# Moving the last four conv-branch tiles of a hybrid trunk layer from the scan's stretch to the Strassen stage ahead of it

## The chip, the cores and the metric

One core of a Trainium2 chip runs the whole program. The metric is the device time of one execution in microseconds (us). TensorE (PE in the rows, its weight loads PEld) multiplies matrices into PSUM; VectorE (DVE), ScalarE (ACT) and GpSimd (POOL) work on tiles of 128 partitions; SyncE (SP) issues most of the loads from memory. Each engine takes its instructions in the order of its own queue.

## The reference, cut to what matters

One layer for 1024 time steps and a model width of 1024, all in float32:

```python
u = rms_norm(x, ln1) * (1 + scale1) + shift1
gl, cb, cc, cx, z, xbc, dt = split(u @ w_in)
y_conv = cb * causal_depthwise_conv(cc * cx, conv_w)       # width 3
p_conv = y_conv @ w_conv_out
xbc = silu(causal_depthwise_conv(xbc, ssm_conv_w) + ssm_conv_b)
xs, bs, cs = split(xbc)                                    # 8 groups
y = ssd_scan(xs * dt, dt * a, bs, cs) + d_skip * xs
y = group_rms_norm(y * silu(z)) * ssm_norm_w
merged = sigmoid(gl_conv) * p_conv + sigmoid(gl_ssm) * (y @ w_ssm_out)
x = x + gate1 * (merged @ w_o)
...
x = x + gate2 * (square(relu(u2 @ w_up)) @ w_down)
```

The conv branch is y_conv: three projections of u (cb, cc, cx, each 1024 channels wide), one product, three taps, one product. In tiles of 128 channels these are eight conv tiles with three projection tiles each.

## The kernel before, in words

Everything lies transposed, channels on partitions and the 1024 time steps along the tile, in two halves of 512. A float32 product is made of three matmuls: each operand is split into a rounded high part (a cast on ScalarE) and the remainder (a subtraction on VectorE), and high x high, high x low and low x high are summed in PSUM. The weights' split is load_w (lines 88 to 95), the three matmuls mm3 (107 to 112), and proj (114 to 121) makes a projection tile of 128 channels from eight blocks of u, 8 x 2 x 3 = 48 matmuls of 512 columns. It takes two of the four PSUM buffers of pool mm.

strassen_pair (134 to 181) makes two projection tiles at once by a Strassen scheme of seven products instead of eight. Each product is 4 blocks x 3 matmuls, so a pair is 84 matmuls where two proj calls are 96. It needs sums of the weights (s12, s34) and of u (the tiles t in X, made once), and hands four quarters of the result, (i, h) for tile i and half h, to a function evac. Their order is (1,1) after four products, (0,0) after five, (0,1) after six and (1,0) after seven.

In order of the program:

1. Norm statistics, modulation, u, and the first six gate tiles (lines 252 to 359).
2. The Strassen stage (425 to 481): ten gate tiles in five pairs, sixteen z tiles in eight pairs, then conv tiles 0 to NYE - 1 = 3. The conv loop at line 456 takes two conv tiles in a round of three pairs: one pair makes cx and cc of the first tile and its product v, one the same for the second, and one makes cb of both. The taps (450 to 454) are one ScalarE and two VectorE instructions. The result lies in two buffers of pool glp (name glt) and is stored to yc_d on ScalarE's queue (481). The tile v has one buffer (name wv), which POOL's memset of two columns opens.
3. The cumulated decays (487 to 506).
4. The scan's stretch (667 to 676). proj_group(g) makes the four projection tiles xs0, xs1, bf and cf of group g through xbc_tile (520 to 532): proj, then raw and cacc with two buffers each, three taps of 1024 columns on VectorE, tanh, one product. ssd_group (546 to 619) runs the scan over eight chunks of 128 steps with small matmuls into A (553 to 556), B (576, 581) and C (598). After the scans of groups 1 to 4, conv_tile (644 to 658) makes conv tiles 4 to 7 with three proj calls each, on tiles ccs and vv of pool pcf, two buffers each, and stores to yc_d.
5. The eight yc_d tiles are reloaded into ccs (683) and split into ys (685), which take the space of u's tiles uh and ul, and so wait for the last projection of group 7. The output projection of the conv branch (693 to 700) runs beside the last scan, then the ssm output projection, w_o, and the MLP.

The engines' orders are not written by hand: a scheduler goes through the program with modelled times and lets an instruction that is ready pass ahead of earlier ones that are not, on each engine. So the projections of group g+1 run on TensorE beside the scan of group g, and the conv tile after them; the scan of group g+1 stands behind both in the program.

Of the kernel before, what the change touches and what calls it, by code (L numbers as in the profile page):

```python
# [5 lines left out]
F32 = mybir.dt.float32  # L6
# [3 lines left out]
ALU = mybir.AluOpType  # L10
# [3 lines left out]
P = 128  # L14
T = 1024
H = 512
# [4 lines left out]
EPS = 1e-6  # L21
RSQRT_SEED = 0x5F3759DF
WARM = 3
NYE = 4
PARTS = ((0, 512, (1, 4, 6)), (512, 256, (1, 3, 4, 6)), (768, 256, (2, 5)))

LN1, LN2, FNORM = 0, 8, 16
# [9 lines left out]
def hybrid_trunk(tc, xT, par, hrows, crow, wada1, wada2, win, wdt, wco, wso, wo, wup, wdn, out):  # L37
    nc = tc.nc
    pe, act, dve, pool, sp = nc.tensor, nc.scalar, nc.vector, nc.gpsimd, nc.sync

    def tt(o, a, b, op, eng=dve):
        return eng.tensor_tensor(out=o, in0=a, in1=b, op=op)  # L42

    def stt(o, a, s, b, op0, op1):
        return dve.scalar_tensor_tensor(out=o, in0=a, scalar=s, in1=b, op0=op0, op1=op1)  # L45
# [4 lines left out]
    hs = [slice(0, H), slice(H, T)]  # L50
# [30 lines left out]
    yc_d = dp.tile([8, P, T], F32, name="yc_d")  # L81

    def load_raw(src):
        raw = wp.tile([P, T], F32, name="wraw", bufs=3)
        sp.dma_start(raw, src)
        return raw

    def load_w(src, raw=None, eng=dve):
        if raw is None:
            raw = load_raw(src)  # L90
        hi = wp.tile([P, T], F32R, name="whi")
        act.copy(hi, raw)  # L92
        lo = wp.tile([P, T], F32R, name="wlo")
        tt(lo, raw, hi.bitcast(F32), ALU.subtract, eng=eng)
        return hi, lo

    def split(hi, lo, src):
        act.copy(hi, src)
        tt(lo, src, hi.bitcast(F32), ALU.subtract)
# [7 lines left out]
    def mm3(outs, wh, wl, xh, xl, start, stop):  # L107
        for o, h_, l_ in zip(outs, xh, xl):
            pe.matmul(o, lhsT=wh, rhs=h_, start=start, stop=False)  # L109
            pe.matmul(o, lhsT=wh, rhs=l_, start=False, stop=False)  # L110
        for o, h_ in zip(outs, xh):
            last_mm[0] = pe.matmul(o, lhsT=wl, rhs=h_, start=False, stop=stop)  # L112

    def proj(w, xh, xl, nk=KT, base=0, halves=(0, 1), width=H):
        wh, wl = w
        ps = [mm.tile([P, H], F32, name="mm")[:, :width] for _ in halves]
        for k in range(nk):
            c0 = base + k * P
            mm3(ps, wh[:, c0:c0 + P], wl[:, c0:c0 + P], [xh[k][h] for h in halves], [xl[k][h] for h in halves],
                k == 0, k == nk - 1)  # L120
        return ps
# [121 lines left out]
    uh = [[up.tile([P, H], F32R, name=f"uh{k}{h}") for h in (0, 1)] for k in range(KT)]  # L243
    ul = [[up.tile([P, H], F32R, name=f"ul{k}{h}") for h in (0, 1)] for k in range(KT)]
# [140 lines left out]
    def sm(name):  # L385
        return p0d.tile([P, C2], F32, name=name)
# [4 lines left out]
    v = sm("v")  # L391
# [58 lines left out]
    def taps(o, v, f):  # L450
        w0 = CONVW + 3 * f
        act.mul(o, v[:, 2:2 + T], prm[:, w0 + 2:w0 + 3])
        for j in (1, 0):
            stt(o, v[:, j:j + T], prm[:, w0 + j:w0 + j + 1], o, ALU.mult, ALU.add)

    for f0 in range(0, NYE, 2):
        ys_ = []
        for f in (f0, f0 + 1):
            y = glp.tile([P, T], F32, name="glt")
            v = pe1.tile([P, T + 32], F32, name="wv", bufs=1)  # L460
            pool.memset(v[:, 0:2], 0.0)
            keep = {}

            def v_ev(i, h, src):
                if (i, h) == (1, 1):
                    keep[0] = src
                elif (i, h) == (0, 0):
                    act.copy(y[:, hs[0]], src)
                else:
                    tt(v[:, 2 + H * h:2 + H * h + H], src, keep[0] if h else y[:, hs[0]], ALU.mult)  # L470

            strassen_pair(pe1, win[17 + 3 * f], win[16 + 3 * f], X, v_ev)
            taps(y, v, f)
            ys_.append(y)

        def y_ev(i, h, src):
            tt(ys_[i][:, hs[h]], src, ys_[i][:, hs[h]], ALU.mult)

        strassen_pair(pe1, win[18 + 3 * f0], win[21 + 3 * f0], X, y_ev)
        for i in (0, 1):  # L480
            act.dma_start(yc_d[f0 + i], ys_[i])
# [5 lines left out]
    with tc.issue_after(last_mm[0].ins):  # L487
# [8 lines left out]
        v = p0e.tile([P, C2], F32, name="v")  # L496
# [18 lines left out]
    pcf = tc.alloc_tile_pool(name="pcf", bufs=2, reuse_waits="tile")  # L515
# [18 lines left out]
    def proj_group(g):  # L534
        pg = p2g[g % 2]
        xs = pg.tile([P, 2, T], F32, name="xs")
        bf = pg.tile([P, T], F32, name="bf")
        cf = pg.tile([P, T], F32, name="cf")
        b = gtile(g)
        xbc_tile(b + 0, 2 * g, xs[:, 0, :])  # L540
        xbc_tile(b + 1, 2 * g + 1, xs[:, 1, :])
        xbc_tile(b + 2, 16 + g, bf)
        xbc_tile(b + 3, 24 + g, cf)
        return xs, bf, cf
# [96 lines left out]
        tsc(r, r, 0.5, None, ALU.mult, ALU.bypass)  # L641
        act.dma_start(rst_d[4 * i:4 * i + 4].rearrange("g (c t) -> (g c) t", t=P), r)

    def conv_tile(f):
        ccs = pcf.tile([P, T], F32, name="ccs")
        v = pcf.tile([P, T + 2], F32, name="vv")
        pool.memset(v[:, 0:2], 0.0)
        cps = proj(load_w(win[16 + 3 * f]), uh, ul)
        for h in (0, 1):
            act.copy(ccs[:, hs[h]], cps[h])  # L650
        xps = proj(load_w(win[17 + 3 * f]), uh, ul)
        for h in (0, 1):
            tt(v[:, 2 + H * h:2 + H * h + H], xps[h], ccs[:, hs[h]], ALU.mult)
        taps(ccs, v, f)
        bps = proj(load_w(win[18 + 3 * f]), uh, ul)
        for h in (0, 1):
            tt(ccs[:, hs[h]], bps[h], ccs[:, hs[h]], ALU.mult)
        act.dma_start(yc_d[f], ccs)

    def drive(gen):  # L660
        try:
            next(gen)
            return None
        except StopIteration as e:
            return e.value
# [3 lines left out]
    for g in range(NG - 1):  # L669
        gen = ssd_group(g, *cur, prev)  # L670
        prev = None
        while prev is None:
            prev = drive(gen)
        cur = proj_group(g + 1)
        if g in (1, 2, 3, 4):
            conv_tile(NYE + g - 1)
    up.release()

    yy = tc.alloc_tile_pool(name="yy", bufs=8, side="right", reuse_waits="tile")
    yc = []  # L680
    for f in range(8):
        ccs = pcf.tile([P, T], F32, name="ccs")
        sp.dma_start(ccs, yc_d[f])
        y = yy.tile([P, 2, T], F32R, name="ys")
        split(y[:, 0, :], y[:, 1, :], ccs)
        yc.append(y)
# [145 lines left out]
    for b in range(8):  # L832
# [21 lines left out]
        else:  # L854
            ws = [load_w(wdn[b, i]) for i in range(4)]
            for t0, tw, onpool in PARTS:
                h, o = t0 // H, t0 % H
# [88 lines left out]
```

## Time and profile before

| | us |
|---|---|
| median of 3 runs | 2210.38 (2208.82 to 2211.97) |
| the profiled execution | 2212.64 |
| its span, first to last instruction | 2210.9 |
| mean granted TensorE clock | 0.979 of full |
| TensorE busy | 2128.2 (96%) |
| VectorE busy | 1410.2 (64%) |
| ScalarE busy | 877.0 (40%) |

A busy column adds up the time in which at least one instruction of the engine runs. Consecutive matmuls overlap in the record, so a count of matmuls in a stretch says more of TensorE's rate than its busy time. In a window's row, the number behind the x is how many instructions the busy time belongs to; PEclk is the granted clock as a share of full. In a row of lines, the fields behind the bar are the total busy time, the mean of one in ns, and the engine's idle time before them with what ended it. In a row of waits: who waited, for whom, the total in us, how many times, the longest.

### The profile page before, as it was taken

The page shows a single profiled execution, that of the slowest core. Times are in us where ns is not written, and L with a number is a line of the kernel's source. Part 1 is how long each engine was busy: PE and PEld are TensorE (multiplying, and loading weights), DVE is VectorE, ACT ScalarE, POOL GpSimd, SP SyncE. Part 2 cuts the span into 40 slices and gives each one's busy share as a digit, 9 for nine tenths or more (in the row PEclk, how much of TensorE's full clock was granted, in tenths as well). Part 3 has the DMA queues.
Part 4 walks back from the last instruction along what each step waited for, and adds up shares of the span by engine and source line. Part 5 has one row for each costly group of instructions (what it writes and reads, how often), then busy time and mean ns, then how long its engine had stood idle before and what let it go on. Part 6 is the DMA issues. An engine that isn't in the chain of part 4 may idle for free.

```text
span 2210.9 us, 26067 instructions
## 1 busy us (share of the span) xinstructions
PE 2128.2 (96%) x9930; PEld 1737.4 (79%) x9930; DVE 1410.2 (64%) x2137; ACT 877.0 (40%) x1449; POOL 145.7 (7%) x216
## 2 busy tenths in 40 slices
PE   5989999999999999999999699999999999999998
PEld 3768778888888888888878488888788888888887
DVE  8957787664787757667884647736755554544444
ACT  4523333324565646455663321234444443211112
POOL 5100000000000000000000000021100000000003
PEclk7989999999999999999999799999999999999998
DMA  7325554223133233233356535553333236332212
GB/s 242 116 77 200 197 184 142 77 76 118 63 99 105 81 97 93 76 113 86 100 180 236 191 105 163 169 184 108 119 113 106 105 112 240 106 105 86 86 39 77
DMA packets 112015, 274.88 MB, mean 124 GB/s; under 512 B 10081, under 2 KB 45281, under 8 KB 111890
## 3 DMA queue, kind: packets, MB, share of 16 engines
q1 hardware_dynamic: 84578, 182.83, 25.9%
q0 software_dynamic: 16192, 58.73, 7.7%
q10 hardware_dynamic: 11120, 31.66, 3.7%
q8 instruction: 78, 1.28, 0.2%
q14 instruction: 47, 0.39, 0.1%
HBM read 214.26 MB, written 58.92 MB: 124 GB/s over the span
## 4 chain that ended last, share of the span: by engine, by line
PE 79%; issue 11%; DVE 6%; DMA 2%; POOL 1%; ACT 1%; SPq 0%; DVEq 0%; POOLq 0%; ACTq 0%
PE mm L143 21%; PE mm L109 17%; PE mm L110 17%; PE mm L112 17%; PE B L576 1%; PE B L581 1%; DVE x L45 1%; PE C L598 1%; DMA yr<-y_d 1%; DMA wv<-in_wada 1%; PE A L553 1%; DVE wada L284 1%; DVE ul L45 1%; POOL wv L422 0%; DVE yr L45 0%
## 5 line engine op out<-in xcount | busy, mean ns | idle before, releaser
L110 PE MATMUL mm<-ul,whi 128*128 128x512 f32 x768 | 305.2, 397 | 6.6 <-DVE ul L45 6.6
L143 PE MATMUL mm<-t,whi 128*128 128x512 f32 x944 | 293.6, 393 | 15.6 <-ACT whi L148 12.5
L109 PE MATMUL mm<-uh,whi 128*128 128x512 f32 x768 | 303.4, 397 | 2.5 <-ACT whi L92 2.5
L92 ACT CAST whi<-wraw 128x1024 fp32r<-128x1024 f32 x126 | 132.3, 1051 | 434.0 <-PE mm L110 410.1
L112 PE MATMUL mm<-uh,wlo 128*128 128x512 f32 x768 | 246.3, 396 | 0.1
L42 DVE TENSOR_TENSOR wlo<-wraw,whi 128x1024 fp32r<-128x1024 f32 (+1 forms) x188 | 212.0, 1128 | 53.0 <-ACT whi L92 46.8
L143 PEld LDWEIGHTS mm<-t,whi 128*128 128x128 f32 x944 | 178.7, 190 | 55.5 <-ACT whi L148 13.3
L45 DVE SCALAR_TENSOR_TENSOR y<-mm,mcol,y 128x512 f32<-128x512 f32 (+1 forms) x136 | 92.5, 716 | 160.0 <-PE mm L112 160.0
L143 PE MATMUL mm<-t,wlo 128*128 128x512 f32 x472 | 183.5, 390 | 0.0
L110 PEld LDWEIGHTS mm<-ul,whi 128*128 128x128 f32 x768 | 145.2, 189 | 36.5 <-DVE ul L45 7.2
L109 PEld LDWEIGHTS mm<-uh,whi 128*128 128x128 f32 x768 | 144.9, 189 | 34.1 <-ACT whi L92 3.3
L112 PEld LDWEIGHTS mm<-uh,wlo 128*128 128x128 f32 x768 | 144.8, 189 | 30.4 <-DVE wlo L42 0.5
L109 PE MATMUL mm<-ys,whi 128*128 128x512 f32 x384 | 148.5, 398 | 10.2 <-ACT s L739 9.7
L110 PE MATMUL mm<-hid,whi 128*128 128x512 f32 (+1 forms) x416 | 155.5, 375 | 0.0
L109 PE MATMUL mm<-hid,whi 128*128 128x512 f32 (+1 forms) x416 | 154.6, 375 | 0.0
L110 PE MATMUL mm<-ys,whi 128*128 128x512 f32 x384 | 149.7, 397 | 0.0
L45 DVE SCALAR_TENSOR_TENSOR cacc<-raw,hw,cacc 128x1024 f32<-128x1024 f32 x96 | 122.7, 1278 | 28.1 <-ACT cacc L528 26.2
L143 PE MATMUL mm<-s,whi 128*128 128x512 f32 x448 | 137.8, 389 | 0.7 <-ACT cu L166 0.7
L112 PE MATMUL mm<-hid,wlo 128*128 128x512 f32 (+1 forms) x416 | 130.5, 374 | 0.0
L112 PE MATMUL mm<-ys,wlo 128*128 128x512 f32 x384 | 123.0, 393 | 0.0
L570 ACT ACTIVATE seg<-acb,acum 128x128 f32<-128x128 f32 x256 | 81.9, 392 | 102.7 <-PE B L576 92.5
L42 DVE TENSOR_TENSOR wlo<-s,whi 128x1024 fp32r<-128x1024 f32 x66 | 80.5, 1220 | 56.2 <-ACT whi L148 56.2
(269 smaller groups left out, 4030.5 us busy)
## 6 DMA issues: line engine op xcount, KB each, us to landing
wraw<-in_win SPq DMA_DIRECT2D x88, 512.0 KB, 3.6
wv<-in_wada POOLq DMA_DIRECT2D x32, 512.0 KB, 3.8
acb<-ac_d SPq DMA_DIRECT2D x64, 256.0 KB, 4.7
wraw<-in_wup SPq DMA_DIRECT2D x32, 512.0 KB, 3.6
hr<-hid_d POOLq DMA_DIRECT2D x32, 512.0 KB, 4.6
wraw<-in_wdn SPq DMA_DIRECT2D x32, 512.0 KB, 3.6
hid_d<-hid POOLq DMA_DIRECT2D x28, 512.0 KB, 4.0
gt<-gl_d SPq DMA_DIRECT2D x24, 512.0 KB, 4.0
```

The source lines that it names most:

```text
L42: return eng.tensor_tensor(out=o, in0=a, in1=b, op=op)
L45: return dve.scalar_tensor_tensor(out=o, in0=a, scalar=s, in1=b, op0=op0, op1=op1)
L92: act.copy(hi, raw)
L109: pe.matmul(o, lhsT=wh, rhs=h_, start=start, stop=False)
L110: pe.matmul(o, lhsT=wh, rhs=l_, start=False, stop=False)
L112: last_mm[0] = pe.matmul(o, lhsT=wl, rhs=h_, start=False, stop=stop)
L143: last_mm[0] = pe.matmul(o, lhsT=l_[:, s_], rhs=r_, start=first and k == j == 0, stop=k == 3 and j == 2, skip_group_check=True)
L284: dve.tensor_tensor_reduce(out=w_, in0=w_, in1=cb, scale=0.5, scalar=prm[:, BADA + o:BADA + o + 1], op0=ALU.mult, op1=ALU.add, accum_out=m ...
L553: pe.matmul(A[:, 0:P], lhsT=bf[:, cs], rhs=cf[:, cs], start=True, stop=True)
L570: act.activation(seg[:, r, :], acb[:, r, :], AF.Relu, bias=acum[:, c, hd:hd + 1], scale=-1.0)
L576: pe.matmul(Bk[o:o + 64, P * (r // 2):P * (r // 2) + P], lhsT=xd[:, r, :], rhs=seg[:, r, :], start=True, stop=True, skip_group_check=True)
L581: pe.matmul(Bk[:, 256 + P * q:256 + P * q + P], lhsT=state[:, 2 * q:2 * q + 2, :].rearrange("p r k -> p (r k)"), rhs=cf[:, cs], start=True ...
```

## The change

NYE and conv_tile go. The Strassen loop over conv tiles runs over all eight, in four rounds in place of two, and the scan's loop calls nothing but the scan and the next group's projections. Pool pcf then holds the tile ccs alone, with three buffers in place of two, for the reloads of yc_d.

```diff
--- before.py
+++ after.py
@@ -21,7 +21,6 @@
 EPS = 1e-6
 RSQRT_SEED = 0x5F3759DF
 WARM = 3
-NYE = 4
 PARTS = ((0, 512, (1, 4, 6)), (512, 256, (1, 3, 4, 6)), (768, 256, (2, 5)))
 
 LN1, LN2, FNORM = 0, 8, 16
@@ -453,7 +452,7 @@
         for j in (1, 0):
             stt(o, v[:, j:j + T], prm[:, w0 + j:w0 + j + 1], o, ALU.mult, ALU.add)
 
-    for f0 in range(0, NYE, 2):
+    for f0 in range(0, 8, 2):
         ys_ = []
         for f in (f0, f0 + 1):
             y = glp.tile([P, T], F32, name="glt")
@@ -641,22 +640,6 @@
         tsc(r, r, 0.5, None, ALU.mult, ALU.bypass)
         act.dma_start(rst_d[4 * i:4 * i + 4].rearrange("g (c t) -> (g c) t", t=P), r)
 
-    def conv_tile(f):
-        ccs = pcf.tile([P, T], F32, name="ccs")
-        v = pcf.tile([P, T + 2], F32, name="vv")
-        pool.memset(v[:, 0:2], 0.0)
-        cps = proj(load_w(win[16 + 3 * f]), uh, ul)
-        for h in (0, 1):
-            act.copy(ccs[:, hs[h]], cps[h])
-        xps = proj(load_w(win[17 + 3 * f]), uh, ul)
-        for h in (0, 1):
-            tt(v[:, 2 + H * h:2 + H * h + H], xps[h], ccs[:, hs[h]], ALU.mult)
-        taps(ccs, v, f)
-        bps = proj(load_w(win[18 + 3 * f]), uh, ul)
-        for h in (0, 1):
-            tt(ccs[:, hs[h]], bps[h], ccs[:, hs[h]], ALU.mult)
-        act.dma_start(yc_d[f], ccs)
-
     def drive(gen):
         try:
             next(gen)
@@ -672,14 +655,12 @@
         while prev is None:
             prev = drive(gen)
         cur = proj_group(g + 1)
-        if g in (1, 2, 3, 4):
-            conv_tile(NYE + g - 1)
     up.release()
 
     yy = tc.alloc_tile_pool(name="yy", bufs=8, side="right", reuse_waits="tile")
     yc = []
     for f in range(8):
-        ccs = pcf.tile([P, T], F32, name="ccs")
+        ccs = pcf.tile([P, T], F32, name="ccs", bufs=3)
         sp.dma_start(ccs, yc_d[f])
         y = yy.tile([P, 2, T], F32R, name="ys")
         split(y[:, 0, :], y[:, 1, :], ccs)
```

## Rows read from the trace of the kernel before

**Rows 1.** The page: the span, and the engines' busy time.
```profile
span 2210.9 us, 26067 instructions
...
PE 2128.2 (96%) x9930; PEld 1737.4 (79%) x9930; DVE 1410.2 (64%) x2137; ACT 877.0 (40%) x1449; POOL 145.7 (7%) x216
```

**Rows 2.** Windows: us, then each engine's busy time, granted clock, DMA share, GB/s.
```profile
core 0: us, PE busy (x) PEld busy (x) DVE busy (x) ACT busy (x) POOL busy (x), PEclk, DMA share, GB/s
400.00:500.00 100.00, 100.00 (x443) 82.81 (x442) 66.09 (x84) 28.63 (x34) 0.30 (x3) 1.00 0.23 74
...
572.00:680.00 108.00, 108.00 (x596) 87.63 (x594) 91.50 (x168) 66.15 (x143) 1.87 (x10) 1.00 0.26 81
723.30:817.96 94.66, 94.66 (x489) 76.77 (x487) 63.43 (x109) 48.43 (x97) 1.56 (x7) 1.00 0.29 90
817.96:912.65 94.69, 94.69 (x489) 76.80 (x487) 63.47 (x109) 48.43 (x97) 1.46 (x6) 1.00 0.29 89
912.65:1007.35 94.70, 94.70 (x489) 76.81 (x488) 65.97 (x121) 48.42 (x97) 1.46 (x6) 1.00 0.32 101
...
1070.00:1110.00 40.00, 40.00 (x220) 32.69 (x219) 35.16 (x63) 25.68 (x53) 0.20 (x2) 1.00 0.28 81
1110.00:1160.00 50.00, 45.67 (x244) 35.76 (x243) 41.70 (x75) 34.04 (x67) 1.06 (x2) 0.97 0.57 192
1230.00:1275.00 45.00, 25.02 (x91) 18.72 (x90) 29.39 (x39) 15.38 (x20) 1.06 (x2) 0.73 0.52 181
```

**Rows 3.** Lines in one period of the scan with a conv tile, 817.96 to 912.65.
```profile
L110 PE MATMUL mm<-ul,whi 128*128 128x512 f32 x112 | 44.3, 396 | 0.0
...
L42 DVE TENSOR_TENSOR wlo<-wraw,whi 128x1024 fp32r<-128x1024 f32 x7 | 8.5, 1220 | 2.2 <-ACT whi L92 2.0
...
L45 DVE SCALAR_TENSOR_TENSOR ccs<-vv,prm,ccs 128x1024 f32<-128x1024 f32 x2 | 2.6, 1284 | 0.2 <-ACT ccs L452 0.2
...
L42 DVE TENSOR_TENSOR vv<-mm,ccs 128x512 f32<-128x512 f32 x2 | 1.3, 686 | 4.5 <-PE mm L112 4.5
L42 DVE TENSOR_TENSOR ccs<-mm,ccs 128x512 f32<-128x512 f32 x2 | 1.3, 686 | 5.7 <-PE mm L112 5.7
```

**Rows 4.** Waits between 520 and 1120 us: total, times, longest.
```profile
ACT whi L92 <- PE mm L110: 85.4, 26, 8.1
...
PEld B L576 <- issue: 16.5, 48, 0.4
...
PEld C L633 <- DVE sql L42: 1.7, 1, 1.7
```

**Rows 5.** Windows, same columns: the two Strassen rounds of conv tiles 0 to 3.
```profile
396.10:510.90 114.80, 114.80 (x508) 95.05 (x507) 77.55 (x98) 33.28 (x40) 0.63 (x7) 1.00 0.24 78
```

**Rows 6.** Tile yc_d: its stores, who waited for its reloads, its DMAs.
```profile
L481 ACTq DMA_DIRECT2D yc_d<-glt x4: 326/326/327, 454.5 to 512.7; - x4
L658 ACTq DMA_DIRECT2D yc_d<-ccs x4: 349/350/350, 714.4 to 997.9; - x4
...
  ACT ys L98: 6.5, 6
...
DMA to landing us min/median/max: 3.4/4.0/4.6
```

**Rows 7.** Lines between 572 and 680 us, scans of groups 0 and 1.
```profile
L112 PE MATMUL mm<-uh,wlo 128*128 128x512 f32 x116 | 36.9, 397 | 0.0
L45 DVE SCALAR_TENSOR_TENSOR cacc<-raw,hw,cacc 128x1024 f32<-128x1024 f32 x24 | 30.6, 1277 | 4.0 <-ACT cacc L528 4.0
...
L42 DVE TENSOR_TENSOR seg<-seg,smk 128x512 f32<-128x512 f32 x14 | 9.5, 681 | 0.1
```

## The prediction

> **What bounds the kernel now.** I read the page first: the span is 2210.9 us and TensorE shows 96% busy [rows 1]. A modelled matmul's busy time overlaps its neighbour's, so busy alone proves little; I therefore read the two stretches that the change touches as windows [rows 2]. Look at the count of matmuls there, not at the busy column. In 400 to 500 us, inside the Strassen work on the conv tiles, TensorE starts 443 matmuls of 512 columns in 100 us, one per 100/443 = 0.2257 us, at full granted clock, with VectorE 66% and ScalarE 29% busy. That is what a TensorE-bound stretch reads in this kernel.
>
> The scan's stretch repeats: with a conv tile in it, one group takes 94.69 us, then 94.70 us [rows 2]. mm3's three lines start 112 matmuls each in it, 336 in all (one of the three is shown) [rows 3]. 336 x 0.2257 = 75.8 us, which leaves 94.7 - 75.8 = 18.9 us for the scan's own small matmuls and what stands between them. The list of waits from 520 to 1120 us shows the direction: ScalarE waited 85.4 us for TensorE's projections, while TensorE's own largest entry is 16.5 us in 48 pieces put down to issue, and the largest that another engine caused is 1.7 us [rows 4]. So the scan's stretch is bound by TensorE too, at VectorE 63.47/94.69 = 67%. The table of windows shows where it is not: 1110 to 1160 us and 1230 to 1275 us, where TensorE is 45.67 of 50 and 25.02 of 45 us busy [rows 2].
>
> **What the change does, part by part.** *Removed from the scan's stretch:* four conv tiles. Each is three projections of 48 matmuls, 144, so 144 x 0.2257 = 32.5 us of TensorE if TensorE stays the bound, 130.0 us for four. With each tile go, on VectorE, three weight splits (3 x 1.220), two products into vv (2 x 0.686), two taps (2 x 1.284) and two products into ccs (2 x 0.686), 9.0 us [rows 3]; on ScalarE three weight casts, two copies and a tap; on SP's queue three weight loads, on ScalarE's queue one store, on POOL's a memset of two columns. None of these sets the end today: VectorE's share is 67%, ScalarE's 48.43/94.69 = 51%. I cost their removal at nothing beyond TensorE's part.
>
> *Added ahead of the scan:* two more rounds of the Strassen loop, for tiles 4 to 7. A round is three pairs of seven products of 12 matmuls, 252, so two rounds are 504 x 0.2257 = 113.8 us. The existing two rounds measure it directly: 396.1 to 510.9 us is 114.8 us with 508 matmuls, VectorE 77.55 us and ScalarE 33.28 us [rows 5], which gives 113.9 us for 504. Splits, sums, taps and evacuations lie beside the matmuls there (VectorE 68%). If that cover were gone, a round would cost VectorE's 77.55/2 = 38.8 us, still less than its 56.9 us of matmuls. The loads are the same twelve weights on SP's queue, one load per 114.8/12 = 9.6 us. The two rounds add four POOL memsets; each waits for the previous tile's taps, as in the present rounds, and behind the last one stand the memsets of the scan's first raw tiles, as now. A new round writes the two glt buffers that the round before is storing. The DMAs of yc_d land 3.4 to 4.6 us after issue [rows 6], and the first write is ScalarE's copy after five of seven products, 60 x 0.2257 = 13.5 us into the round; so nothing waits, as at the one such seam now.
>
> *The third ccs buffer, no vv:* of the eight reloads of yc_d three instead of two can be ahead of time. ScalarE waited 6.5 us in six pieces for these reloads [rows 6], while VectorE and the last scan chunks ran beside it; bounds 0 to 6.5 us of gain, and I take 0, since the last of the eight is still behind ys splits that need the space of uh and ul.
>
> *The pace of the scan without its filler* is the unknown that decides. By TensorE a group then needs 192 x 0.2257 + 18.9 = 62.2 us. VectorE needs 63.47 - 9.0 = 54.5 us of it, 88%; ScalarE, even with all of today's 48.43 us, 78%. No row shows a long run at 88%, but one is close: 572 to 680 us, the scans of groups 0 and 1 before any conv tile. There lie 3 x 116 = 348 projection matmuls, 24 cacc taps (two groups' worth) and 14 masked segments of a group's 8 [rows 7]: 348/192 = 1.81 groups of projections and 14/8 = 1.75 of scan, almost exactly the mix that the change leaves. At 62.2 us these would take 109 to 113 us; they took 108, with VectorE 91.50/108 = 85% busy and TensorE unbroken [rows 2]. A second such piece, 1070 to 1110 us, runs VectorE at 35.16/40 = 88%, TensorE again unbroken [rows 2]. So I take 62.2 us, and bounds of 60 us (108/1.8) and 68.1 us. The upper one is 54.5/0.80, two points of VectorE's share under the split of gain and loss worked out below, and five under what 572 to 680 us reached.
>
> **Sum.** -130.0 + 113.8 = -16.2 us (72 matmuls fewer). Against the profiled execution, 2212.6 us with a span of 2210.9, that is 2196.4; its 2212.6 is 2.2 us over the median of 2210.4, so against the median I forecast **2194.2 us**. With the bounds of pace over four groups, 4 x (60 - 62.2) = -8.8 and 4 x (68.1 - 62.2) = +23.6, it runs from 2185.4 to 2217.8; the likeliest case's own range is 2188 to 2200.
>
> **Rivals.** *The filler covered idle TensorE time.* The weight loads' share is 82.81% in the Strassen stretch and 76.80/94.69 = 81.1% in a scan period [rows 2]. Read as slack, the scan period holds (1 - 81.1/82.8) x 94.7 = 1.9 us in which TensorE did nothing, and 4 x 1.9 = 7.8 us of the removed matmuls come back as gaps: 2194.2 + 7.8 = 2202. For it: the small matmuls swap weights often, and the 16.5 us of issue. Against it: 572 to 680 us is not slower than the sum. The Trainium skill, Perfetto Trace Analysis, section Identifying the Most-Contended Engine, says that matmul busy time does not tell how near TensorE is to its limit and that the share of LDWEIGHTS does; by it the 83% of the Strassen stretch would itself be 17% headroom. The trace disagrees on that last point: 443 matmuls in 100 us is the steadiest rate the kernel shows, so 83% is the ceiling for this mix and only the difference of the two shares is slack.
>
> *VectorE becomes the bound (slower).* Place: the four periods that lose their conv tile. VectorE's 54.5 us must fit in the period; the gain of 16.2 us over four groups is 4.05 us each, so it turns into a loss when the period passes 66.3 us, that is when VectorE cannot hold more than 54.5/66.3 = 82%. At 80% each period is 68.1 us, +5.9 us, in all +23.6 - 16.2 = +7.4 us, 2217.8; at 78%, 69.9 us a period, 2225. What would do it: the taps of a projection keep their two raw and two cacc buffers, ScalarE cannot empty PSUM, and TensorE waits behind it in order with the scan's matmuls queued after. For it: the conv tile is the one filler with little VectorE work (9.0 us against 32.5 us of matmuls), and VectorE has room to catch up in it. Against it: 85% and 88% in the two rows above. The Trainium skill, same page, section Optimization Strategy, says that where the most contended engine changes between regimes, interleaving the regimes may help, which is what the present kernel does and the change undoes; by it this rival would be the outcome. The trace does not show two regimes with different bounds here, since TensorE is unbroken in both.
>
> *The change shifts the tail.* The stalls of 1110 to 1160 us and 1230 to 1275 us, 4.3 and 20.0 us of TensorE, at granted clocks of 0.97 and 0.73 of full [rows 2], depend on how the end of the last scan meets the output projections. If the new order lets scan 7 fall back by about one group's taps, the second stall grows by some 15 us and the result is about 2209, no change.
>
> **How the numbers follow.** Forecast 0.62 (2188 to 2200); slack 0.17 (about 2202); VectorE bound 0.13 (2215 to 2225); tail 0.08 (about 2209). A measurement of this kernel can tell about 0.2%, 4.4 us, from no change. The first two are faster by more: 0.79; the tail case is within: 0.08; VectorE bound is slower, its price at 80% being 7.4 us: 0.13. The range 2188 to 2213 takes in the first, second and last case and the pace's bounds up to that rival; it leaves out the VectorE case and the end of the pace's bounds below 2188, together under 2 in 10.
>
> **What the profile after would show.** Right: 12 Strassen pairs back to back from about 396 to 625 us with 443 matmuls per 100 us; scan groups 62 us apart with 192 projection matmuls each; VectorE near 88% there, TensorE without waits for VectorE or ScalarE; the last projection of group 7 ending some 16 us earlier than now. Wrong: groups 66 us or more apart, ScalarE's copies into raw waiting for VectorE's cacc and TensorE's projections waiting for PSUM; granted clock under 1.00 inside the scan; or a longer stall before the second half of the output projections.

## The result, and the profile after

The changed kernel takes **2223.22 us** (median of four runs, 2222.07 to 2225.27) where the kernel before took 2210.81 beside it: 1.0061 of it, with an interval of 1.0048 to 1.0073. It is 12.4 us slower; 2194.2 had been forecast, so 29.0 us are to be explained. The page of the changed kernel, answering to [rows 1]:

```profile
span 2220.3 us, 26029 instructions
...
PE 2117.5 (95%) x9858; PEld 1728.1 (78%) x9858; DVE 1453.6 (65%) x2203; ACT 883.9 (40%) x1463; POOL 146.0 (7%) x216
```

TensorE has the 72 matmuls less. Windows of the changed kernel, columns as in [rows 2]: the Strassen rounds of the conv tiles, the scan's long middle, three short stretches, and the tail.

```profile
core 0: us, PE busy (x) PEld busy (x) DVE busy (x) ACT busy (x) POOL busy (x), PEclk, DMA share, GB/s
...
396.10:624.90 228.80, 228.80 (x1011) 189.43 (x1010) 156.62 (x200) 66.08 (x78) 0.84 (x9) 1.00 0.23 76
690.00:950.00 260.00, 260.00 (x1407) 209.67 (x1406) 212.42 (x380) 164.41 (x350) 5.03 (x24) 1.00 0.31 89
950.00:975.00 25.00, 18.49 (x109) 14.52 (x109) 19.36 (x42) 17.02 (x40) 1.07 (x2) 0.90 0.40 122
1075.00:1100.00 25.00, 22.02 (x128) 17.22 (x126) 14.30 (x31) 13.63 (x29) 0.00 (x0) 0.99 0.35 97
1100.00:1125.00 25.00, 9.58 (x38) 7.38 (x37) 23.03 (x37) 18.18 (x33) 1.07 (x2) 0.64 0.58 199
1250.00:1300.00 50.00, 29.99 (x115) 22.83 (x114) 20.16 (x28) 14.77 (x22) 1.07 (x2) 0.76 0.37 125
```

The added Strassen rounds came as forecast: 1011 matmuls in 228.8 us, 442 per 100 us, and 114.0 us more than the two rounds of [rows 5]. The tail stands idle for 50 - 29.99 = 20.0 us, the same 20.0 as before [rows 2]. The loss lies between. From 690 to 950 TensorE shows not one gap, yet it then stands for 6.5 us in 950 to 975, 3.0 in 1075 to 1100 and 15.4 in 1100 to 1125, 24.9 us in all where the kernel before lost 4.3 in 1110 to 1160 [rows 2].

To see what TensorE was doing while it was busy, these windows are cut at the first small matmul of each scan group and count one of the three projection lines alone, line 111 (columns: us, PE busy and count, PEld busy and count, PEclk, DMA share, GB/s). A projection tile is 16 of these matmuls, a group needs 64. The first row lies ahead of scan 0, the second is scan 0:

```profile
625.00:685.30 60.30, 25.90 (x84) 15.77 (x84) 1.00 0.40 135
685.30:742.80 57.50, 20.25 (x62) 11.59 (x62) 1.00 0.22 64
742.80:801.70 58.90, 19.16 (x62) 11.66 (x62) 1.00 0.36 103
801.70:869.60 67.90, 24.14 (x72) 13.40 (x72) 1.00 0.33 95
869.60:943.00 73.40, 27.50 (x83) 15.61 (x84) 1.00 0.32 92
943.00:1008.40 65.40, 18.76 (x54) 10.49 (x54) 0.95 0.34 97
1008.40:1080.60 72.20, 25.61 (x79) 14.84 (x79) 1.00 0.33 96
1080.60:1159.90 79.30, 20.06 (x58) 11.47 (x58) 0.87 0.49 169
```

The count behind PE's busy time is the thing to read: 3.9 tiles in each of scans 0 and 1, then 4.5 and 5.2. In 801.7 to 943.0 TensorE makes 155/16 = 9.7 tiles while two groups of scan pass, which need 8. It is busy, and a growing part of its work is for later groups; the groups stretch to 73.4 us.

The sum of these counts, over 16, less 4 for each earlier group, is the lead with which the projections enter a group; 4.0 means that just the group's own four tiles are made. For groups 2 to 6 it is 5.0, 5.5, 6.7, 6.1 and 7.0. In the kernel before, a period with a conv tile held 112/16 = 7 tiles, 4 and the conv tile's 3 [rows 3], and counted in the same way, conv tiles taken off, the lead was 4.0 at the start of each of groups 2 to 5.

How that run-ahead is paid shows in the waits of the changed kernel between 640 and 1130 us (total, times, longest), where [rows 4] had no entry over 1.7 us of TensorE for another engine:

```profile
PEld mm L108 <- ACT cacc L527: 16.4, 2, 11.4
PE mm L108 <- ACT cacc L527: 16.0, 2, 11.1
...
ACT xs L530 <- DVE zs L41: 9.6, 3, 5.6
```

And in its timeline (start, duration, instruction, in brackets the idle time before it), first around 970, then around 1110 us:

```profile
963.46 2.35 DVE L41 TENSOR_TENSOR zs<-xs,zs 128x1024 f32<-128x1024 f32 x2
...
966.77 1.99 ACT L530 ACTIVATE xs<-cacc 128x1024 f32<-128x1024 f32 x2
...
972.40 1.44 ACT L527 ACTIVATE cacc<-mm,hb,hw 128x512 f32<-128x512 f32 x2
...
973.23 0.79 PE L108 MATMUL mm<-uh,whi 128*128 128x512 f32 x1 [4.85 <-ACT cacc L527]
...
1103.61 2.35 DVE L41 TENSOR_TENSOR zs<-xs,zs 128x1024 f32<-128x1024 f32 x2
...
1109.46 1.04 ACT L97 CAST ys<-ccs 128x1024 fp32r<-128x1024 f32 x1 [4.89 <-DMA ccs<-yc_d]
...
1111.65 2.00 ACT L530 ACTIVATE xs<-cacc 128x1024 f32<-128x1024 f32 x2
...
1120.04 2.78 ACT L527 ACTIVATE cacc<-mm,hb,hw 128x512 f32<-128x512 f32 x4
...
1120.87 0.80 PE L108 MATMUL mm<-ys,whi 128*128 128x512 f32 x1 [11.13 <-ACT cacc L527]
1121.46 0.63 PE L109 MATMUL mm<-ys,whi 128*128 128x512 f32 x1
1121.88 0.63 PE L111 MATMUL mm<-ys,wlo 128*128 128x512 f32 x1
```

Read each part from the top. A group's xs has two buffers, so the tanh that writes group 5's waits for the last product (zs) of scan 3. Until then the cacc tiles stay full, ScalarE cannot empty the projections' PSUM, and TensorE's next projection stands, with the scan's matmuls queued behind it. The same at 1103, with scan 5 and group 7, where the matmul that stands is the first of the output projection (mm<-ys), and there ScalarE also stands 4.89 us for a reload of yc_d, with that tanh behind it. By then the projections of u are used up: the last matmul of them started at 1094.2, when 13 of the last two scans' 16 chunks had not begun. In the kernel before it started at 1114.9 with 8 to go. From 1094 until the output projection starts, what is left of the scan has nothing beside it.

### The profile page after: what moved, and what is told of

Its sections match the earlier page's. It is cut to its first block, busy times and chain, and to the rows that moved or that the text cites. A ratio compares the mean times of both kernels' runs of the same rounds, so it can differ in the third digit from the quotient of the medians.

```text
span 2220.3 us, 26029 instructions
## 1 busy us (share of the span) xinstructions
PE 2117.5 (95%) x9858; PEld 1728.1 (78%) x9858; DVE 1453.6 (65%) x2203; ACT 883.9 (40%) x1463; POOL 146.0 (7%) x216
## 4 chain that ended last, share of the span: by engine, by line
PE 83%; issue 7%; DVE 5%; DMA 2%; ACT 1%; POOL 1%; SPq 0%; DVEq 0%; POOLq 0%; ACTq 0%
PE mm L142 28%; PE mm L108 16%; PE mm L111 16%; PE mm L109 16%; PE B L575 2%; PE B L580 1%; DVE x L44 1%; PE C L597 1%; PE A L552 1%; DVE wada L283 1%; DVE ul L44 1%; DMA yr<-y_d 0%; DMA ccs<-yc_d 0%; POOL wv L421 0%; PE A L555 0%
## 5 line engine op out<-in xcount | busy, mean ns | idle before, releaser
L142 PE MATMUL mm<-t,whi 128*128 128x512 f32 x1136 | 352.5, 392 | 14.6 <-ACT whi L147 11.5
L91 ACT CAST whi<-wraw 128x1024 fp32r<-128x1024 f32 x114 | 119.7, 1051 | 378.8 <-PE mm L109 339.0
L142 PEld LDWEIGHTS mm<-t,whi 128*128 128x128 f32 x1136 | 214.5, 189 | 62.3 <-ACT whi L147 12.6
L109 PE MATMUL mm<-ul,whi 128*128 128x512 f32 x576 | 229.2, 398 | 6.9 <-DVE ul L44 6.9
L108 PE MATMUL mm<-uh,whi 128*128 128x512 f32 x576 | 228.1, 400 | 7.3 <-ACT cacc L527 4.8
L142 PE MATMUL mm<-t,wlo 128*128 128x512 f32 x568 | 220.7, 390 | 0.0
L111 PE MATMUL mm<-uh,wlo 128*128 128x512 f32 x576 | 189.4, 398 | 0.1
L108 PEld LDWEIGHTS mm<-uh,whi 128*128 128x128 f32 x576 | 109.1, 190 | 31.7 <-ACT cacc L527 5.0
L147 ACT CAST whi<-wraw 128x1024 fp32r<-128x1024 f32 x78 | 65.2, 837 | 154.7 <-PE mm L142 140.7
L111 PEld LDWEIGHTS mm<-uh,wlo 128*128 128x128 f32 x576 | 108.8, 190 | 22.8 <-DVE wlo L41 0.5
L142 PEld LDWEIGHTS mm<-t,wlo 128*128 128x128 f32 x568 | 106.9, 188 | 22.3
```

Source lines behind the costliest of these rows:

```text
L142: last_mm[0] = pe.matmul(o, lhsT=l_[:, s_], rhs=r_, start=first and k == j == 0, stop=k == 3 and j == 2, skip_group_check=True)
```

## The experiments

Three theories stood. **O**, the order: without the conv tiles the projections get ahead of the scan in TensorE's queue, and the two-buffered tiles turn that into stalls. **V**: VectorE is too full, the prediction's slower rival. **E**: the loss is made at the end, where reloads, splits and the last scan meet. In the later expectations OV is VectorE's load acting in part through the order. Except where another base is named, the edits are made to the changed kernel.

**1. Hold the order.** An issue edge keeps each projection of group g behind a named chunk's C matmul of an earlier scan:

```diff
+HOLD = (3, 5, 0, 2)
...
-        ps = proj(load_w(win[win_i]), uh, ul)
+        w = load_w(win[win_i])
+        if behind in scan_mm:
+            with tc.issue_after(scan_mm[behind].ins):
+                ps = proj(w, uh, ul)
...
+        xbc_tile(b + 0, 2 * g, xs[:, 0, :], (g - 2, HOLD[0]))
+        xbc_tile(b + 1, 2 * g + 1, xs[:, 1, :], (g - 2, HOLD[1]) if HOLD[1] > 0 else (g - 1, 0))
+        xbc_tile(b + 2, 16 + g, bf, (g - 1, HOLD[2]))
+        xbc_tile(b + 3, 24 + g, cf, (g - 1, HOLD[3]))
...
                 last = pe.matmul(C, lhsT=bt, rhs=xe.rearrange("p r k -> p (r k)"), start=True, stop=True)
+                scan_mm[g, c] = last
```

> The changed kernel, with the matmuls of each projection tile held in TensorE's order behind a named chunk of the scan, so that projections stay about 4.4 tiles ahead of the scan at each group's start instead of drifting from 4.5 to 6.4; the work of every engine is the same. Theory O (order: TensorE spends the scan's share on projections that come too early, the two-group buffers fill, and at the end the scan is left over without company): the stalls at 965 to 973 us and 1096 to 1121 us go, and the time is 2194 to 2202 us. Theory V (VectorE's work binds the scan, whatever the order): groups stay 65 to 73 us apart, TensorE's idle time turns up spread through the scan, and the time is 2215 us or more. Theory E (only the end is at fault: reloads of yc_d and the ys splits stand in front of the last group's taps): the stall at 1096 to 1121 us stays and the time is 2215 to 2223 us.

Measured: 2205.62 us, 0.9978 of the kernel before (0.9969 to 0.9988); 17.6 us of the 29 are back. The time lies above O's range and below V's and E's. The two stalls are gone, and the projections no longer run ahead: exactly four tiles in each of groups 2 to 5. Two windows of this kernel by scan group, columns as in [rows 2], and its largest waits of TensorE for another engine:

```profile
803.30:868.10 64.80, 61.93 (x342) 49.87 (x341) 54.22 (x99) 41.65 (x91) 1.46 (x6) 1.00 0.33 94
868.10:933.40 65.30, 64.14 (x347) 50.95 (x346) 53.79 (x101) 42.27 (x92) 1.46 (x6) 0.98 0.36 101
```

```profile
PE B L583 <- DVE t L42: 5.1, 5, 1.6
...
PE C L605 <- ACT row L642: 4.4, 3, 1.8
```

Groups of some 65 us, not 62.2 (64.0 to 66.3 in groups 2 to 5): small waits remain, for VectorE's sums t and for a row of ScalarE's. Two of the waits for t, 1.65 and 1.64 us before 865.45 and 994.93, follow a weight split of 1.22 us that stands ahead of t in VectorE's queue (863.09 and 992.57). O holds for most of the loss, not for all.

**2. Take the weight splits of the scan's projections from VectorE, with no edge in the order.** The weights' subtraction goes to GpSimd, a memset of three columns the other way:

```diff
-        ps = proj(load_w(win[win_i]), uh, ul)
+        ps = proj(load_w(win[win_i], eng=pool), uh, ul)
-        pool.memset(raw[:, 0:3], 0.0)
+        dve.memset(raw[:, 0:3], 0.0)
```

> The changed kernel, with the weight splits of the scan's own projections (four per group, 1.22 us each) on GpSimd in place of VectorE, where one takes about 2.6 us, and raw's small memset on VectorE in place of GpSimd; TensorE's order still lets the projections drift ahead, from 4.8 to 6.0 tiles at a group's start. Theory V: VectorE's 54.5 us per group become 49.7 us, 9% less, the scan's groups move from 65 to 73 us apart to 60 to 66 us, and the time is 2193 to 2203 us. Theory O: the order is the same, so the two stalls stay, and the time is 2214 to 2224 us. Theory E: the same, 2214 to 2224 us.

Measured: 2208.19 us in one run, between the theories: 15 us back with no edge in the order. It does not speak for V alone, for two reasons. The order moved too: counted as above, the lead at the starts of groups 2 to 5 is 5.0, 5.0, 5.5 and 6.5, so the drift sets in a group later. And VectorE was hardly relieved: it is busy 52.8 us a group over groups 0 to 5 (316.96/6), 54.5 in the changed kernel (327.26/6), where 49.7 had been expected. The last section shows why.

**3. Cut VectorE's taps**, which leaves two of the three VectorE taps of each scan projection out of the computation:

```diff
-        for j in (2, 1, 0):
+        for j in (2,):
```

> The changed kernel with two of the three VectorE taps of each scan projection left out (8 x 1.278 = 10.2 us per group; the convolution of the scan's inputs is then incomplete). TensorE's order then keeps the projections 4.3 tiles ahead at every group's start. Theory O and theory V both expect 2188 to 2198 us with no stall inside the scan. Theory E expects the stall of some 20 us after the last projection to stay, and 2212 us or more.

Measured: 2193.68 us in one run, the forecast's 2194.2 to within a us. Neither the reloads nor their splits were edited, so E falls as the main cause, as far as this edit can say: the last group's taps were cut too. Two windows of this kernel by scan group:

```profile
803.10:865.70 62.60, 62.60 (x345) 49.98 (x343) 45.22 (x91) 42.27 (x91) 1.46 (x6) 1.00 0.36 101
865.70:928.20 62.50, 62.50 (x344) 49.89 (x343) 45.22 (x91) 42.26 (x91) 1.47 (x6) 1.00 0.35 102
```

This is the pace that the prediction took, 62.2 us a group. O is not excluded by it: the lead of the projections, counted in the trace as above, stays at 4.8 to 5.0 tiles through groups 0 to 6, where the changed kernel's grows to 7.0. (The expectations count the lead in another way and put it some half a tile lower.) Less work on VectorE also keeps the order.

**4. Two conv tiles back, after scans 3 and 6**, so 2 where the kernel before has 4 in the scan; conv_tile and two ccs buffers come back with them:

```diff
+NYE = 6
...
-    for f0 in range(0, 8, 2):
+    for f0 in range(0, NYE, 2):
...
         cur = proj_group(g + 1)
+        if g in (3, 6):
+            conv_tile(NYE + (3, 6).index(g))
```

> The changed kernel with six conv tiles in the Strassen stage and two back in the scan's stretch as plain tiles, after the scans of groups 3 and 6, so that one of them lies between the last own projection and the output projections. TensorE has 2 x (32.5 - 28.5) = 8.1 us more to do. Theory O: the tile after group 3 gives the scan time to catch up and the one after group 6 covers the leftover scan, both stalls go, and the time is 2223 + 8 - 28 = 2203 us (2197 to 2209). Theory V: the two tiles relieve VectorE in two of seven groups, so about 2/7 of the lost 28 us come back, 2223 + 8 - 8 = 2223 us (2216 to 2226). Theory E: the stall after the last projection is covered, 20 us of the 28: 2211 us (2207 to 2214).

Measured: 2211.75 us in one run. It lies in E's range and just past the end of O's. Both large stalls are gone, but 8.3 of 50 us are idle in 1110 to 1160, so it does not separate the two by itself. What it shows of the order: the lead, 5.5 tiles at the start of group 3 as in the changed kernel, is back at 4.0 at the start of group 4, behind the conv tile.

**5. Both edits, 1 and 2.**

> Both edits together: projections held behind the scan's chunks, and their weight splits on GpSimd. Holding the order alone gave 2205.6 us, with groups 57.5 to 69.9 us apart where TensorE's work needs 62.2; the splits alone gave 2208.2 us. Theory OV (what is lost is VectorE's load, partly through the order that it brings about and partly as waits of the scan for VectorE): with the order held and VectorE at 49.7 us per group the scan runs at TensorE's pace, and the time is 2194 to 2200 us. Theory W (what is left after holding is the wait for the one buffer C around the squares' sum of the group before, which no relief of VectorE shortens): 2203 to 2207 us.

Measured: **2198.34 us** (2196.46 to 2200.8), 0.9948 of the kernel before (0.9931 to 0.9964): faster than both kernels, and in OV's range. Three of its windows by scan group, then two with one projection line alone (columns as above):

```profile
802.20:863.40 61.20, 61.19 (x334) 49.04 (x333) 53.67 (x95) 40.40 (x86) 13.44 (x7) 1.00 0.33 97
925.30:987.80 62.50, 62.43 (x345) 49.86 (x344) 55.42 (x100) 42.55 (x93) 13.00 (x7) 1.00 0.35 102
987.80:1049.70 61.90, 61.90 (x345) 49.72 (x343) 58.35 (x113) 42.46 (x93) 11.17 (x6) 1.00 0.37 105
```

```profile
802.20:863.40 61.20, 20.68 (x64) 12.02 (x64) 1.00 0.33 97
863.40:925.30 61.90, 20.74 (x64) 11.73 (x64) 1.00 0.34 103
```

Exactly four tiles a group, groups of 61.2 to 62.5 us, and TensorE all but unbroken. VectorE is busy 88 to 94% of the group (53.67/61.20 to 58.35/61.90), not the 49.7 us that the expectation took; some 6 us of each group are instructions that stand beside GpSimd (last section). The waits for t are down from 5.1 to 0.5 us between 640 and 1130 us. That the splits' place in VectorE's queue is what edit 2 mended in run 1 is the likely reading; no run tests it by itself. The last scan's zs product starts at 1222.3; it was 1237.5 in the kernel before and 1249.2 in the changed one.

**6. The third ccs buffer taken away.**

```diff
-        ccs = pcf.tile([P, T], F32, name="ccs", bufs=3)
+        ccs = pcf.tile([P, T], F32, name="ccs")
```

> The changed kernel with two buffers of ccs in place of three; nothing else. Theory OV: the end's stall is the leftover scan, so the time stays within 3 us of 2223. Theory E (the early reloads of yc_d and the ys splits that they let through stand in front of the last group's taps): the stall after the last projection shrinks by 5 us or more, 2218 us or less.

Measured: 2218.86 us in one run, 4.4 less, between the two ranges: where the end is jammed, the third buffer, costed at nothing, was a loss. TensorE's longest wait there falls from 11.4 to 5.7 us. That is E's share. With edits 1 and 2 in, taking it away did not help:

> Held projections, splits on GpSimd, and two buffers of ccs in place of three. hold_and_pool gave 2198.3 us with groups 62 us apart; the third buffer alone cost the changed kernel 4.4 us (2218.9 with two). If it costs that wherever it stands: 2192 to 2196 us. If it cost it only because the end was jammed there: within 2 us of 2198.3.

Measured: 2201.97 us (2199.33 to 2205.57), 3.6 more than run 5, which neither expectation had. The runs of the two overlap, so the sign of these 3.6 us is not settled; a gain of 4.4 us is not there.

**7. One more tap's work on VectorE**, 32 times, in the kernel before and in the changed one:

```diff
+        stt(a, raw[:, 0:T], 0.0, a, ALU.mult, ALU.add)
         act.activation(dst, a, AF.Tanh)
```

> The kernel before, with one more VectorE tap in each scan projection, a product with zero that leaves the values as they are: 4 x 1.278 = 5.1 us of VectorE per group. Theory OV: in the periods with a conv tile VectorE has 31 us of 94.7 to spare, so the extra work costs nothing in the four periods that have one, and at most some us in the groups without: 2210 to 2216 us. If VectorE were as tight in the kernel before as in the changed one, it would cost 7 x 5.1 = 36 us, 2246 us.

> The changed kernel with the same extra tap: VectorE's demand becomes 59.6 us in a period that TensorE needs 62.2 us for, 96%. Theory OV: with relief of 10.2, 4.9 and 0 us per group the loss against 2194 us was 0, 14 and 29 us, about 2.9 us for each us of VectorE in a group; 5.1 us more give 15 to 36 us more, 2238 to 2259 us. Theory E: the extra work lies beside TensorE's except at the end, 2223 to 2230 us.

Measured, one run each: 2211.96 before (+1.0) and 2233.19 after (+10.0). The kernel before has room on VectorE for some 32 x 1.28 = 41 us of work; the changed one has not. The size lies between E's range and OV's 15 to 36. The stall is now spread over four groups: TensorE stands for 6.8, 7.4, 6.0 and 9.7 us around 907, 980, 1050 and 1120.

**8. Edit 2 on the kernel before**, for whether it is worth having by itself.

> The kernel before with the same two lines as split_on_pool: the splits of the scan's own projections on GpSimd, raw's memset on VectorE. Theory OV: VectorE is not tight there (67% in a period with a conv tile), so its relief buys nothing: 2208 to 2213 us. If the relief were good by itself wherever it stands, it would bring what it brought in the changed kernel, 15 us: 2193 to 2199 us.

Measured: 2213.79 us, 1.0013 of the kernel before (1.0003 to 1.0022), just above the range of theory OV. The same lines that give 15 us in the changed kernel give nothing here. So this edit alone, without the move of the conv tiles, is not what makes run 5 faster; the issue edges were not tried on the kernel before.

## Why the prediction was wrong

- **The sum of removed and added matmuls** was right. The rounds took 114.0 us where 113.8 had been summed, and the 130 us did leave the scan's stretch: the last projection came 20.7 us earlier than before, where some 16 had been forecast. That mark was met and meant little, since the scan had fallen behind the projections.
- **The step that failed** is "So I take 62.2 us". Its support, 572 to 680 us, covers groups 0 and 1 only, and there the two kernels' orders are alike: both enter group 0 with 5.25 and group 1 with 5.1 tiles of lead, and the changed kernel ran group 1 in 58.9 us. The drift begins at group 2, and groups 2 to 5 took 65.4 to 73.4 us. A long run was needed, and the only rows of one had conv tiles in it.
- **The inference under it failed too**: TensorE unbroken was read as the scan keeping pace. From 690 to 950 it was unbroken while a group went from 58.9 to 73.4 us. In the kernel before the conv tile stood between the projections of g+1 and the scan of g+1 (its place in the program) and cost VectorE 9.0 us in 32.5. It held the lead at 4.0 tiles, and run 4 shows one conv tile bring it back there; that it also gave the scan's chain time is argued from these two figures. Costing "their removal at nothing beyond TensorE's part" overlooked that.
- **The pace itself was right** as what TensorE can do: 61.4 to 62.8 us in groups 2 to 5 with taps cut, 61.2 to 62.5 with edits 1 and 2.
- **The slower rival** had the sign and the size (2217.8 to 2225; measured 2223.2), and its chain, cacc to PSUM to TensorE, is the one in the timeline. Its condition, VectorE holding no more than 82%, is what the long run reads: 212.42/260 = 82% in 690 to 950 us, and 82 to 84% in run 1's groups (53.79/65.30 and 54.22/64.80); the rows of 85 and 88% that spoke against it were short. That VectorE can hold no more is not shown: run 1 gets 17.6 us back with the same work on VectorE. Run 5's 88 to 94% does not show the contrary either, since it counts the time in which instructions stood. The rival's chain bites at two places, when the projections have run two groups ahead. Order and VectorE's queue act together: run 1 gives 17.6 us, run 2 gives 15.0, both 24.9, less than their sum. The rule of the Trainium skill, Perfetto Trace Analysis, section Optimization Strategy, that interleaving regimes may help, was set aside because TensorE was unbroken in both. The measured sign is the rule's, though it gives no size and no row shows that the most contended engine changes.
- **Slack and tail.** Run 5 shows TensorE all but unbroken without filler (61.19 of 61.20 us), so the slack rival finds no support. The tail's stall is unchanged at 20.0 us.
- **The third ccs buffer at 0** with a bound of 6.5 us on the gain's side alone: it cost 4.4 us in the jammed end (run 6, one run). The bound should have had both signs.

The ledger of the 29.0 us, from the two pages: TensorE's idle time grew by 20.1 us (2210.9 - 2128.2 = 82.7 to 2220.3 - 2117.5 = 102.8), and its busy time fell by 10.7 us instead of 16.2. Of these 5.5 us an estimated 2.5 are the clock's: after the two large stalls 19 matmuls start 0.43 us apart instead of 0.2257 (1121.46 and 1121.88 in the timeline), where the kernel before has 7 such, and 12 x 0.2 = 2.5. The last 3.4 us are only where the profiled executions lie, 2.2 above the median before and 1.2 below it after. So 3 us stay without a place. With both edits in, the forecast's sum held: run 5's profiled execution took 2196.5 us, against the 2196.4 summed for a profiled execution, with 2194.7 - 2111.4 = 83.3 us of TensorE idle. It is the fastest of four; their median of 2198.3 is 4 us over 2194.2. Open is why the scheduler's order drifts with what stands in VectorE's queue: its modelled times are not in the record.

## What to carry to other kernels

A busy engine may be busy with the wrong work: where a producer and a consumer share an in-order queue, count the producer's tiles per step of the consumer, and look for the buffers that end the run-ahead. Work that looks like filler can be the brake that keeps the two in step, so when it is taken out, pin the order and shorten the next-busiest engine's queue in the same edit (here 2198.3 where the bare change gave 2223.2). After moving work between engines, look whether the busy time of the one that gave it away fell by what was moved. A row that is to stand for the pace of a long stretch must come from late enough in it for a drift to show.

## What the runs showed of the hardware that had not been expected

Work that GpSimd took over did not leave VectorE much shorter. Run 5 moved 32 splits of 1.22 us, 39 us, and by its page VectorE's busy time fell by 9.1 us (1453.6 to 1444.5):

```profile
PE 2111.4 (96%) x9858; PEld 1723.2 (79%) x9858; DVE 1444.5 (66%) x2203; ACT 885.5 (40%) x1463; POOL 228.9 (10%) x216
```

GpSimd made the subtraction at 2.70 us against VectorE's 1.22 [rows 3], and most of VectorE's instructions with both operands in SBUF that started while it ran stood until it was done. Two lines of run 5 between 640 and 1100 us (total busy, mean ns, idle time before with what ended it), then one meeting of the two in its timeline:

```profile
L42 POOL TENSOR_TENSOR wlo<-wraw,whi 128x1024 fp32r<-128x1024 f32 x28 | 75.6, 2702 | 315.9 <-ACT whi L92 281.2 <-PE C L640 24.2 <-PE B L583 8.1
L45 DVE SCALAR_TENSOR_TENSOR bf<-bf,cacc 128x1024 f32<-128x1024 f32 x8 | 16.3, 2040 | 1.6 <-ACT bf L538 1.6
```

```profile
847.25 2.48 POOL L42 TENSOR_TENSOR wlo<-wraw,whi 128x1024 fp32r<-128x1024 f32 x1 [8.09 <-ACT whi L92]
847.40 3.42 DVE L45 SCALAR_TENSOR_TENSOR bf<-bf,cacc 128x1024 f32<-128x1024 f32 x1
```

The product for bf takes 1222 ns in the mean of run 1; here it took 3.42 us and ended 1.09 us after the subtraction. Instructions that read PSUM were not held: xd, xe and t keep a mean of 411 to 415 ns in run 5. In the four groups from 802 to 1050 us the lengthening adds up to an estimated 24 us, 6 a group, more than the four splits that had left the group (4 x 1.22 = 4.9). So VectorE's 94% in a group of 61.9 us is not 94% of work.

And a stall costs more than its length: the granted clock was 0.64 of full in 1100 to 1125 us, with matmuls at about half their rate just after the gap, as at the lower of the two clock levels (1.2 for 2.4 GHz).
